# A fused decoder layer on one core: GpSimd's arithmetic given to VectorE and ScalarE, and ten chunks of x_m taken from the unnormalised input

## The chip, the cores and the metric

One core of a Trainium2 chip runs the whole layer in one launch. The core's engines run side by side, each through its own queue in order: TensorE (PE in the profile, PEld its weight loads), VectorE (DVE), ScalarE (ACT), GpSimd (POOL), and SyncE (SP), which here issues nearly all DMA transfers. The metric is the device time of one execution in microseconds (us), lower is better.

## What is computed

The layer normalises its input x (512 x 1024, float32), projects it with one matrix of 12288 columns, and feeds two branches: an attention over three dilated windows and an mLSTM with a causal convolution in front. Both are projected back, gated, added, projected once more and added to x, with a final RMSNorm. Cut to what the change touches:

```
xn = rmsnorm(x, norm_in_g)                       # x * rsqrt(mean(x*x) + eps) * g, a factor per token
q_a, k_a, v_a, z_a, x_m, z_m, o_m, gates = split(xn @ w_in)
# mLSTM branch
x_c  = silu(causal_depthwise_conv(x_m))          # 4 taps along time
q, k = block_diag_proj(x_c, wq), block_diag_proj(x_c, wk)     # blocks of 4 channels
v    = block_diag_proj(x_m, wv)
gate_pre = concat(q, k, v) @ w_if + b_if         # 8 columns: input and forget gates of 4 heads
h = mlstm_chunkwise(q, k, v, gates from gate_pre)
# attention branch: 16 heads of 64, scores q.k / 8 + bias(distance), softmax, times v
```

The factor of the normalisation belongs to a token, and tokens lie along the free axis of the projections that are held transposed. So the projection may also be made from x times the gain, and the result multiplied by the factor of each token.

## The kernel before

**Matmuls.** Every projection is made in three matmuls per 128 x 128 block: both operands are split into a high part (h, rounded to the fp32r format) and a low part (l, the rest), and hi*hi, hi*lo and lo*hi are added up in PSUM (`mm3`). For a chunk of 128 output channels a weight tile of 128 x 1024 is loaded (`raw`, 512 KB), ScalarE makes `whi`, VectorE makes `wlo` (`halves`), and TensorE runs 8 blocks x 3 matmuls of 512 columns. There are four buffers of each of raw, whi and wlo.

**Start.** x comes transposed in eight tiles `xt`. `x_split(k)` makes `xh` (ScalarE) and `xl` (VectorE) from xt and the gain. The first four chunks of x_m (`EARLY`) are taken from these unnormalised parts, `xu`, while the squares of x are summed and the token factors spread over the partitions into `rb` (a part of the tile `norm`). Then GpSimd multiplies the eight xt by rb, x_split runs on them again, and everything else uses these normalised parts `xh`, `xl`. The four early chunks are multiplied by rb when VectorE takes them out of PSUM; later chunks of x_m are copied out by ScalarE.

**The x_m loop** (16 chunks ct, four to a head). Per chunk: x_m to SBUF (tile `xm`) and to DRAM (`xmd`), a convolution of four steps on VectorE (`conv`: one tensor_scalar, three scalar_tensor_tensor), tanh on ScalarE (`cth`), one more VectorE step, the split (`xch`, `xcl`), a scaled copy (`sx`), then on TensorE `kp` (three matmuls with the folded matrix M of the q and k blocks, `Mh`, `Ml`), its split (`kph`, `kpl`, `kf`) and the products `S` (nine matmuls of 512, 384 and 256 columns and a small one). After each fourth chunk come 16 pairs of small matmuls `gates`, which need x_m and the convolution of all four.

**GpSimd's arithmetic before.** The eight products xt by rb; the folding of gate weights (`wrep`, `ust` in `fold_gates`), of `wqrep` and `mrow` (`fold_rows`), of `M` and `Bv` (`spread`, once per head each); in attention, per pair of heads, two copies of `qh` and two of `ql` to the other half of the partitions; and memsets and one cast, which stay.

**Order.** Nothing is written in the final order. `Recorder` notes every instruction with its inputs and outputs and then plays them through a list scheduler with its own costs per instruction: on each engine the ready instruction with the smallest priority goes first. Priority is the place in the program minus `R.ahead`, so a larger R.ahead pulls work forward (weights run 300 places ahead). The scheduled order is then fixed on each engine. Since one helper records everything, all lines of the profile read L333; the tiles' names tell the instructions apart. In the order, `x8` stands for eight like instructions in a row.

Of the kernel before, what the change touches and what calls it, by code (L numbers as in the profile page):

```python
# [11 lines left out]
F32 = mybir.dt.float32  # L12
F32R = mybir.dt.float32r
I32 = mybir.dt.int32
AF = mybir.ActivationFunctionType
OP = mybir.AluOpType

P = 128
T = 512
NT = T // P  # L20
D = 1024
NK = D // P
MW = 2048
NMT = MW // P
# [7 lines left out]
CQ, CK, CV, CZA, CXM, CZM, COM, CG = 0, 8, 16, 24, 32, 48, 64, 80  # L32
# [305 lines left out]
def hybrid_layer(ctx, tc, a, out):  # L338
    nc = tc.nc
    R = Recorder(nc, a["win"].tensor)  # L340
    V, A, PE, G, SP = (R.engine(e) for e in ("vector", "scalar", "tensor", "gpsimd", "sync"))
# [11 lines left out]
    def slot(name, dt=F32):  # L353
        return tile_of(upool, [P, 516], dt, name, "u", NSLOT)
# [24 lines left out]
    def dram(name, shape):  # L379
        return R.buf(lambda: dpool.tile(shape, F32, name=name), shape, F32, dram=True)  # L380

    def mm3(ps, lh, ll, rh, rl, first, last):
        PE.matmul(ps, lh, rh, start=first, stop=False)
        PE.matmul(ps, lh, rl, start=False, stop=False)
        PE.matmul(ps, ll, rh, start=False, stop=last)
# [42 lines left out]

    ident = const("ident", [P, P], F32)
    pc = const("pc", [P, PC_N], F32)  # L430
    EARLY = 4
    pair = [wide("xt") for _ in range(NK // 2)]
    xt = [pair[k // 2][:, k % 2 * T:k % 2 * T + T] for k in range(NK)]

# [9 lines left out]
    def proj_k(ps, hl, x, k):  # L444
        c = slice(k * P, (k + 1) * P)
        mm3(ps, hl[0][:, c], hl[1][:, c], *x[k], k == 0, k == NK - 1)
# [18 lines left out]
    xu = []  # L465
    early_ps = [mm_bank("xm") for _ in range(2)]
# [21 lines left out]
    norm = wide_t("norm", F32)  # L488
    rb, dg, ones = norm[:, :T], norm[:, T:2 * T], norm[:, 2 * T:2 * T + P]
# [17 lines left out]
    for c in range(2, EARLY):  # L507
# [2 lines left out]
        early_ps.append(sc_bank("xm"))  # L510
        for k in range(NK):
            proj_k(early_ps[c], early[c], xu, k)
    R.ahead = 1000
    xh, xl = [], []
    for k in range(NK):
        G.tensor_mul(xt[k], xt[k], rb)
        h, l = x_split(k)
        xh.append(h)
        xl.append(l)
    R.ahead = 0  # L520

    def proj_t(chunk, name):
        hl = weights(a["win"][chunk])
        ps = mm_bank(name)
        for k in range(NK):
            c = slice(k * P, (k + 1) * P)
            mm3(ps, hl[0][:, c], hl[1][:, c], xh[k], xl[k], k == 0, k == NK - 1)
        return ps

    def proj_n(chunk, name):  # L530
# [43 lines left out]
    def fold_gates():  # L574
        for m in range(2):
            G.memset(ust[m], 0.0)
        wrep = []
        for n in range(3):
            w = slot("wrep")[:, :512].rearrange("p (c o g) -> p c o g", c=NMT, o=4)
            SP.dma_start(w, a["wrep"][n])  # L580
            G.tensor_mul(w, w, brow[:, n, :, :, None].to_broadcast([P, NMT, 4, 8]))
            wrep.append(w)
        for m, ns in ((0, (0, 1)), (1, (2,))):
            u = ust[m][:, :, :8]
            parts = [wrep[n][:, :, o, :] for n in ns for o in range(4)]
            G.tensor_add(u, parts[0], parts[1])
            for x in parts[2:]:
                G.tensor_add(u, u, x)


    brow = const("brow", [P, 3, NMT, 4])
# [5 lines left out]
    def fold_rows():  # L597
        wq = slot("wqrep")[:, :256].rearrange("p (c i o) -> p c i o", c=NMT, i=4)
        SP.dma_start(wq, a["wqrep"])
        G.tensor_mul(wq, wq, brow[:, 1, :, None, :].to_broadcast([P, NMT, 4, 4]))  # L600
        G.tensor_add(mrow, wq[:, :, :, 0], wq[:, :, :, 1])
        G.tensor_add(mrow, mrow, wq[:, :, :, 2])
        G.tensor_add(mrow, mrow, wq[:, :, :, 3])

    def spread(rows, h, name):
        b = slot(name)[:, :512]
        G.tensor_mul(b.rearrange("p (c g i) -> p c g i", c=4, i=4),
                     rows[:, 4 * h:4 * h + 4, None, :].to_broadcast([P, 4, 32, 4]),
                     bmask[:, None, :, :].to_broadcast([P, 4, 32, 4]))
        return b  # L610
# [7 lines left out]
        return Mh, Ml  # L618

    fold_rows()  # L620
    xmd = dram("xmd", [NMT, P, T])
    sxd = dram("sxd", [NMT, P, T])
    v_of = {}

# [24 lines left out]
    sraw = []  # L649
    for ct in range(NMT):  # L650
        h, c = divmod(ct, 4)
        ps = early_ps[ct] if ct < EARLY else proj_t(CXM + ct, "xm")
        if c == 0:
            Mh, Ml = fold_qk(h)
            sps = [sc_bank("S") for _ in range(3)]
        m = slot("xm")[:, :T + 3]
        V.memset(m[:, 0:3], 0.0)
        if ct < EARLY:
            V.tensor_mul(m[:, 3:], ps, rb)
        else:  # L660
            A.activation(m[:, 3:], ps, AF.Copy)
        SP.dma_start(xmd[ct], m[:, 3:])
        if ct == 8:
            block_v(0)
        xc = conv_silu(m, ct)
# [236 lines left out]
    for p in range(HEADS_A // 2):  # L902
# [6 lines left out]
        for w in range(2):  # L909
            o, o2 = 64 * w, 64 - 64 * w  # L910
            src = qps[o:o + 64]
            A.activation(qh[w][o:o + 64], src, AF.Copy, scale=0.125)
            V.scalar_tensor_tensor(ql[w][o:o + 64], src, 0.125, qh[w][o:o + 64].bitcast(F32),
                                   op0=OP.mult, op1=OP.subtract)
            G.tensor_copy(qh[w][o2:o2 + 64], qh[w][o:o + 64])
            G.tensor_copy(ql[w][o2:o2 + 64], ql[w][o:o + 64])
        kps = proj_t(CK + p, "ka")
        kk = [slot("kk", F32R)[:, :T] for _ in range(2)]
        for w in range(2):
# [227 lines left out]
```

## Time and profile before

| what | value |
|---|---|
| median of 3 runs | 906.77 us (906.05 to 907.6) |
| the profiled execution | 907.21 us, span in the trace 905.2 us |
| TensorE busy | 886.7 us, 98% of the span |
| VectorE busy | 576.0 us, 64% |
| ScalarE busy | 385.8 us, 43% |
| GpSimd busy | 71.5 us, 8% |

The span runs from the first to the last instruction in the trace; the execution's time has about 2 us around it. "Busy" of an engine is the time in which at least one of its instructions runs. TensorE's matmuls overlap, so a row's duration (0.40 us for 512 columns) is longer than the distance to the next start (about 0.23 us), and work is counted by starts.

### The profile page before, as it was taken

Reading aid. Unit: us, or ns where it says so; the run is one execution under the profiler, and the core shown is the slowest. Engines: PE = TensorE matmul, PEld = TensorE weight load, DVE = VectorE, ACT = ScalarE, POOL = GpSimd, SP = SyncE. Lnnn points to the kernel's source line nnn. Section 1 sums busy time; section 2 is a strip of 40 time slices with the busy share of each in tenths; the row PEclk is TensorE's granted clock in tenths of the full one; section 3 lists DMA queues with packets and bytes.
Section 4 is the critical chain, followed back from the end, with each engine's and each line's share of the span. In section 5 each row is a group of like instructions: output and inputs, shape, how many; then the busy total and the mean of one; then the engine's idle time right before and its main releaser. Section 6 shows DMA issues by size and latency. Waiting matters only on the chain.

```text
span 905.2 us, 11844 instructions
## 1 busy us (share of the span) xinstructions
PE 886.7 (98%) x4340; PEld 727.1 (80%) x4340; DVE 576.0 (64%) x1154; ACT 385.8 (43%) x724; POOL 71.5 (8%) x136
## 2 busy tenths in 40 slices
PE   7899999999999999999999999999999999999997
PEld 5577878788878888887888888888888888888886
DVE  4998987785428546744855477874777843328533
ACT  7445544443343332332333265563665543325222
POOL 0950110000000000000000111101011100000000
PEclk9799999999999999999999999999999999999999
DMA  9652334233049234204313222313223223224221
GB/s 305 223 173 99 124 118 161 82 129 105 11 152 341 102 117 163 93 23 162 126 53 124 96 73 105 128 59 104 74 79 105 71 81 101 98 94 157 77 81 59
DMA packets 38801, 104.64 MB, mean 116 GB/s; under 512 B 4308, under 2 KB 6100, under 8 KB 38744
## 3 DMA queue, kind: packets, MB, share of 16 engines
q1 hardware_dynamic: 38600, 103.63, 33.6%
q8 instruction: 34, 0.56, 0.2%
q10 hardware_dynamic: 144, 0.26, 0.1%
q14 instruction: 23, 0.19, 0.1%
HBM read 93.35 MB, written 15.77 MB: 121 GB/s over the span
## 4 chain that ended last, share of the span: by engine, by line
PE 93%; DVE 4%; issue 1%; ACT 1%; DMA 1%; SPq 0%; DVEq 0%; ACTq 0%
PE zm L333 10%; PE gate L333 10%; PE ym L333 10%; PE om L333 9%; PE xm L333 8%; PE out L333 5%; PE qa L333 5%; PE za L333 5%; PE ka L333 5%; PE va L333 5%; PE ya L333 5%; PE num L333 3%; PE S L333 3%; PE pv L333 2%; PE sa L333 2%; PE pT L333 2%
## 5 line engine op out<-in xcount | busy, mean ns | idle before, releaser
L333 DVE TENSOR_TENSOR wlo<-raw,whi 128x1024 fp32r<-128x1024 f32 (+1 forms) x126 | 151.4, 1203 | 159.7 <-ACT whi L333 159.7
L333 ACT ACTIVATE whi<-raw 128x1024 fp32r<-128x1024 f32 (+1 forms) x126 | 128.1, 1019 | 284.7 <-PE zm L333 79.2
L333 PE MATMUL xm<-xh,whi 128*128 128x512 f32 x128 | 54.3, 427 | 5.2 <-ACT whi L333 5.2
L333 PE MATMUL xm<-xl,whi 128*128 128x512 f32 x128 | 54.0, 423 | 2.1 <-DVE xl L333 2.1
L333 PE MATMUL xm<-xh,wlo 128*128 128x512 f32 x128 | 53.2, 418 | 1.7 <-DVE wlo L333 1.7
L333 PE MATMUL om<-wlo,xh 128*128 128x512 f32 x128 | 50.9, 397 | 0.0
L333 PE MATMUL gate<-xh,whi 128*128 128x512 f32 x128 | 50.9, 397 | 0.0
L333 PE MATMUL zm<-xh,whi 128*128 128x512 f32 x128 | 50.8, 397 | 0.0
L333 PE MATMUL gate<-xl,whi 128*128 128x512 f32 x128 | 50.7, 396 | 0.0
L333 PE MATMUL om<-whi,xh 128*128 128x512 f32 x128 | 50.6, 396 | 0.0
L333 PE MATMUL om<-whi,xl 128*128 128x512 f32 x128 | 50.6, 395 | 0.0
L333 PE MATMUL gate<-xh,wlo 128*128 128x512 f32 x128 | 50.6, 395 | 0.0
L333 PE MATMUL ym<-yl,whi 128*128 128x512 f32 x128 | 50.5, 394 | 0.0
L333 PE MATMUL zm<-xl,whi 128*128 128x512 f32 x128 | 50.4, 394 | 0.0
L333 PE MATMUL ym<-yh,wlo 128*128 128x512 f32 x128 | 50.4, 394 | 0.0
L333 PE MATMUL zm<-xh,wlo 128*128 128x512 f32 x128 | 50.4, 394 | 0.0
L333 PE MATMUL ym<-yh,whi 128*128 128x512 f32 x128 | 50.2, 392 | 0.0
L333 ACT ACTIVATE p<-p,mx 128x128 f32<-128x128 f32 (+1 forms) x64 | 35.4, 556 | 14.3 <-DVE mx L333 14.3
L333 DVE CUSTOM_DVE_ANT_0 p<-sa,tb 128x128 f32<-128x128 f32 (+1 forms) x64 | 28.3, 488 | 18.2 <-PE sa L333 18.2
L333 DVE SCALAR_TENSOR_TENSOR conv<-xm,half,conv 128x512 f32<-128x512 f32 x48 | 37.2, 775 | 0.8
L333 DVE TENSOR_TENSOR ymacc<-ymacc,ym 128x512 f32<-128x512 f32 x24 | 16.5, 687 | 31.2 <-PE ym L333 31.2
L333 PEld LDWEIGHTS xm<-xh,whi 128*128 128x128 f32 x128 | 25.8, 201 | 11.6 <-ACT whi L333 5.8
(253 smaller groups left out, 2222.5 us busy)
## 6 DMA issues: line engine op xcount, KB each, us to landing
raw<-in_win_dram SPq DMA_DIRECT2D x94, 512.0 KB, 3.4
raw<-in_wpb_dram SPq DMA_DIRECT2D x16, 512.0 KB, 3.2
fr<-fd SPq DMA_DIRECT2D x1, 5120.0 KB
xmd<-xm SPq DMA_DIRECT2D x16, 256.0 KB, 2.2
sxd<-sx SPq DMA_DIRECT2D x16, 256.0 KB, 2.1
xmr<-xmd SPq DMA_DIRECT2D x16, 256.0 KB, 4.2
sxr<-sxd SPq DMA_DIRECT2D x16, 256.0 KB, 4.1
tb<-fr SPq DMA_DIRECT2D x16, 256.0 KB, 3.7
```

Source lines behind the costliest of these rows:

```text
L333: getattr(getattr(self.nc, op.eng), fn)(*a, **k)
```

## The change

Three things are changed.

First, all arithmetic of GpSimd goes elsewhere: the products xt by rb, the folds and `spread` to VectorE, the copies of qh and ql in attention to ScalarE. GpSimd keeps memsets and one cast.

Second, ten chunks of x_m (`UNNORMED`) instead of four are taken from the unnormalised parts `xu`; VectorE multiplies each by rb on its way out of PSUM. Only the first four (`EARLY`) are still made ahead of the loop, and their way out of PSUM is put forward by R.ahead = 5000.

Third, the normalisation of xt and its second split are no longer done at once: `normalise` is called for two of the eight tiles in each of the loop's turns 5 to 8 (`FIRST` and the three after it). The chunks from the eleventh on, and all later projections, use the normalised parts.

```
-    EARLY = 4
+    EARLY, UNNORMED, FIRST = 4, 10, 5
...
+    def x_m(ct, ps, norm=None):
+        m = slot("xm")[:, :T + 3]
+        V.memset(m[:, 0:3], 0.0)
+        if norm is None:
+            A.activation(m[:, 3:], ps, AF.Copy)
+        else:
+            V.tensor_mul(m[:, 3:], ps, norm)
+        SP.dma_start(xmd[ct], m[:, 3:])
+        return m
+
+    R.ahead = 5000
+    early_m = [x_m(c, early_ps[c], rb) for c in range(EARLY)]
+    R.ahead = 0
     xh, xl = [], []
-    for k in range(NK):
-        G.tensor_mul(xt[k], xt[k], rb)
+
+    def normalise(k):
+        V.tensor_mul(xt[k], xt[k], rb)
         h, l = x_split(k)
         xh.append(h)
         xl.append(l)
-    R.ahead = 0
...
-            G.tensor_mul(w, w, brow[:, n, :, :, None].to_broadcast([P, NMT, 4, 8]))
+            V.tensor_mul(w, w, brow[:, n, :, :, None].to_broadcast([P, NMT, 4, 8]))
...
-            G.tensor_add(u, parts[0], parts[1])
+            V.tensor_add(u, parts[0], parts[1])
...
-        ps = early_ps[ct] if ct < EARLY else proj_t(CXM + ct, "xm")
+        raw_x = ct < UNNORMED
+        ps = None if ct < EARLY else proj_t(CXM + ct, "xm", xu if raw_x else None)
+        if FIRST <= ct < FIRST + NK // 2:
+            normalise(2 * (ct - FIRST))
+            normalise(2 * (ct - FIRST) + 1)
...
+        R.ahead = EMPTY
+        m = early_m[ct] if ct < EARLY else x_m(ct, ps, rb if raw_x else None)
+        R.ahead = 0
...
-            G.tensor_copy(qh[w][o2:o2 + 64], qh[w][o:o + 64])
-            G.tensor_copy(ql[w][o2:o2 + 64], ql[w][o:o + 64])
+            A.activation(qh[w][o2:o2 + 64], qh[w][o:o + 64].bitcast(F32), AF.Copy)
+            A.activation(ql[w][o2:o2 + 64], ql[w][o:o + 64].bitcast(F32), AF.Copy)
```

The same exchange of G for V is made in `fold_rows` and `spread`.

VectorE's queue just behind the spreading of the token factors (`norm<-ident,nz` is the last step of that) stood like this before:

```order
L333 TENSOR_TENSOR xm<-xm,norm 128x512 x3
L333 CAST sel<-selr 36x512
L333 TENSOR_TENSOR rel_380<-relb,rel_380 32x16
L333 SCALAR_TENSOR_TENSOR xl<-xt,pc,xh 128x512
L333 TENSOR_TENSOR wlo<-raw,whi 128x1024
L333 SCALAR_TENSOR_TENSOR xl<-xt,pc,xh 128x512
L333 TENSOR_TENSOR wlo<-raw,whi 128x1024
L333 SCALAR_TENSOR_TENSOR xl<-xt,pc,xh 128x512 x2
L333 TENSOR_TENSOR wlo<-raw,whi 128x1024
L333 SCALAR_TENSOR_TENSOR xl<-xt,pc,xh 128x512 x4
```

and stands like this now, at the same place:

```order
L333 TENSOR_TENSOR xm<-xm,norm 128x512 x3
L333 TENSOR_TENSOR mrow<-wqrep 128x64
L333 TENSOR_SCALAR conv<-xm,half 128x512
L333 TENSOR_TENSOR mrow<-mrow,wqrep 128x64
L333 SCALAR_TENSOR_TENSOR conv<-xm,half,conv 128x512
L333 TENSOR_TENSOR wlo<-raw,whi 128x1024
L333 TENSOR_TENSOR mrow<-mrow,wqrep 128x64
L333 SCALAR_TENSOR_TENSOR conv<-xm,half,conv 128x512
L333 TENSOR_TENSOR xm<-xm,norm 128x512
L333 TENSOR_TENSOR wlo<-raw,whi 128x1024 x2
L333 TENSOR_TENSOR M<-mrow,bmask 128x512
```

The eight xl have gone from here; the first convolution and pieces of the folds have come in their place.

TensorE's queue at the start of the fifth chunk, with what each matmul waits for, stood like this before:

```order
L333 MATMUL xm<-xh,whi 128x512 [waits DVE_49,Activation_49]
L333 MATMUL xm<-xl,whi 128x512 [waits DVE_49]
L333 MATMUL xm<-xh,wlo 128x512 [waits DVE_49]
L333 MATMUL xm<-xh,whi 128x512 [waits Activation_49]
L333 MATMUL xm<-xl,whi 128x512 [waits DVE_49]
L333 MATMUL xm<-xh,wlo 128x512
```

and there it stands like this now:

```order
L333 MATMUL xm<-xh,whi 128x512 [waits DVE_49,Activation_49]
L333 MATMUL xm<-xl,whi 128x512
L333 MATMUL xm<-xh,wlo 128x512 [waits DVE_49]
L333 MATMUL xm<-xh,whi 128x512
L333 MATMUL xm<-xl,whi 128x512
```

The chunk no longer waits block by block for VectorE and ScalarE; it waits once for its weights. In the sixth chunk the first kp comes now, 14 matmuls behind the chunk's start (before, it came in the seventh):

```order
L333 MATMUL xm<-xl,whi 128x512
L333 MATMUL kp<-xch,Mh 128x512 [waits Activation_49]
L333 MATMUL xm<-xh,wlo 128x512
L333 MATMUL xm<-xh,whi 128x512
L333 MATMUL xm<-xl,whi 128x512
L333 MATMUL kp<-xcl,Mh 128x512 [waits DVE_49]
L333 MATMUL kp<-xch,Ml 128x512
```

So chains of the convolution start earlier between the x_m matmuls than before.

## Rows read from the trace of the kernel before

**Rows 1.** The page: busy time by engine, and TensorE's granted clock in 40 slices.

```profile
PE 886.7 (98%) x4340; PEld 727.1 (80%) x4340; DVE 576.0 (64%) x1154; ACT 385.8 (43%) x724; POOL 71.5 (8%) x136
...
PEclk9799999999999999999999999999999999999999
```

**Rows 2.** Windows: length, then busy PE, PEld, DVE, ACT, POOL; PEclk, DMA, GB/s.

```profile
31.53:76.95 45.42, 39.67 (x152) 30.05 (x150) 42.81 (x48) 21.36 (x34) 26.14 (x22) 0.85 0.48 164
76.95:160.00 83.05, 82.73 (x478) 66.71 (x478) 71.56 (x110) 41.23 (x79) 6.56 (x5) 1.00 0.36 128
```

**Rows 3.** The chain that ended last: start, duration in us, what.

```profile
505.29 5.57 PE qa L333 x24
```

**Rows 4.** Waits of TensorE: who for whom, total us, times, longest.

```profile
PE xm L333 <- DVE xl L333: 2.1, 3, 0.8
PE xm L333 <- DVE wlo L333: 1.7, 1, 1.7
PE aT L333 <- DVE aa L333: 0.5, 1, 0.5
```

**Rows 5.** Timeline of TensorE: start, duration in us, instruction, wait before it.

```profile
31.53 0.40 PE L333 MATMUL xm<-xh,whi 128*128 128x512 f32 x1
...
58.08 0.50 PE L333 MATMUL kp<-xch,Mh 128*128 128x512 f32 x1 [1.95 <-ACT xch L333]
...
59.57 0.63 PE L333 MATMUL xm<-xh,whi 128*128 128x512 f32 x1
60.00 0.63 PE L333 MATMUL xm<-xl,whi 128*128 128x512 f32 x1
...
76.95 0.41 PE L333 MATMUL gates<-xm,ust 128*32 128x256 f32 x2
...
100.67 0.41 PE L333 MATMUL gates<-xm,ust 128*32 128x256 f32 x2
```

**Rows 6.** VectorE by shape, 28.6 to 58.74: busy us, mean ns, idle before.

```profile
L333 DVE TENSOR_TENSOR wlo<-raw,whi 128x1024 fp32r<-128x1024 f32 x6 | 11.1, 1845 | 0.0
L333 DVE SCALAR_TENSOR_TENSOR xl<-xt,pc,xh 128x512 fp32r<-128x512 f32 x8 | 9.9, 1282 | 0.0
```

**Rows 7.** The same view of VectorE, 61.8 to 75.9.

```profile
L333 DVE TENSOR_TENSOR wlo<-raw,whi 128x1024 fp32r<-128x1024 f32 x2 | 2.5, 1225 | 0.7 <-ACT whi L333 0.7
```

**Rows 8.** Timeline of GpSimd.

```profile
26.84 13.06 POOL L333 TENSOR_TENSOR xt<-xt,norm 128x512 f32<-128x512 f32 x8 [0.77 <-DMA wrep<-in_wrep_dram]
```

**Rows 9.** Timeline of VectorE, seven instructions in a row while GpSimd rests.

```profile
85.86 0.75 DVE L333 SCALAR_TENSOR_TENSOR conv<-xm,half,conv 128x512 f32<-128x512 f32 x1
86.53 0.68 DVE L333 TENSOR_TENSOR xcl<-conv,xch 128x512 fp32r<-128x512 f32 x1
87.13 1.22 DVE L333 TENSOR_TENSOR wlo<-raw,whi 128x1024 fp32r<-128x1024 f32 x1
88.26 0.69 DVE L333 SCALAR_TENSOR_TENSOR conv<-cth,conv 128x512 f32<-128x512 f32 x1
88.89 0.56 DVE L333 TENSOR_TENSOR kpl<-kp,kph 128x384 fp32r<-128x384 f32 x1
89.36 0.48 DVE L333 TENSOR_SCALAR sx<-conv,hs 128x512 f32<-128x512 f32 x1
89.75 0.68 DVE L333 TENSOR_TENSOR xcl<-conv,xch 128x512 fp32r<-128x512 f32 x1
```

**Rows 10.** Timelines of VectorE and ScalarE before the fifth chunk.

```profile
26.80 1.89 DVE L333 TENSOR_TENSOR xm<-xm,norm 128x512 f32<-128x512 f32 x3 [1.66 <-ACT norm L333]
...
30.05 1.06 ACT L333 ACTIVATE whi<-raw 128x1024 fp32r<-128x1024 f32 x1 [1.16 <-DMA raw<-in_win_dram]
```

**Rows 11.** Attention: GpSimd's copies by shape, then timelines of ScalarE and TensorE.

```profile
L333 POOL CAST qh<-qh 64x512 fp32r<-64x512 f32 x16 | 10.8, 673 | 295.7 <-ACT qh L333 275.1 <-issue 20.1
...
540.42 1.06 ACT L333 ACTIVATE whi<-raw 128x1024 fp32r<-128x1024 f32 x1 [2.24 <-PE ka L333]
...
545.97 0.28 PE L333 MATMUL sa<-kk,qh 128*128 128x256 f32 x1
```

More of the change, by code (lines that the diff above doesn't have):

```diff
@@ L512, in hybrid_layer @@
             proj_k(early_ps[c], early[c], xu, k)
-    R.ahead = 1000
+    xmd = dram("xmd", [NMT, P, T])
+    def x_m(ct, ps, norm=None):
[10 more added lines that the diff above has]
+    R.ahead = 0
     xh, xl = [], []
-    for k in range(NK):
-        G.tensor_mul(xt[k], xt[k], rb)
+    def normalise(k):
+        V.tensor_mul(xt[k], xt[k], rb)
         h, l = x_split(k)
@@ L519, in hybrid_layer, with proj_t @@
         xl.append(l)
-    R.ahead = 0
-    def proj_t(chunk, name):
+    def proj_t(chunk, name, x=None):
         hl = weights(a["win"][chunk])
@@ L525, in proj_t @@
         for k in range(NK):
-            c = slice(k * P, (k + 1) * P)
-            mm3(ps, hl[0][:, c], hl[1][:, c], xh[k], xl[k], k == 0, k == NK - 1)
+            proj_k(ps, hl, x or list(zip(xh, xl)), k)
         return ps
@@ L585, in fold_gates @@
             parts = [wrep[n][:, :, o, :] for n in ns for o in range(4)]
-            G.tensor_add(u, parts[0], parts[1])
+            V.tensor_add(u, parts[0], parts[1])
             for x in parts[2:]:
-                G.tensor_add(u, u, x)
+                V.tensor_add(u, u, x)
     brow = const("brow", [P, 3, NMT, 4])
@@ L599, in fold_rows @@
         SP.dma_start(wq, a["wqrep"])
[L600 to L603, printed above, removed]
+        V.tensor_mul(wq, wq, brow[:, 1, :, None, :].to_broadcast([P, NMT, 4, 4]))
+        V.tensor_add(mrow, wq[:, :, :, 0], wq[:, :, :, 1])
+        V.tensor_add(mrow, mrow, wq[:, :, :, 2])
+        V.tensor_add(mrow, mrow, wq[:, :, :, 3])
     def spread(rows, h, name):
         b = slot(name)[:, :512]
-        G.tensor_mul(b.rearrange("p (c g i) -> p c g i", c=4, i=4),
+        V.tensor_mul(b.rearrange("p (c g i) -> p c g i", c=4, i=4),
                      rows[:, 4 * h:4 * h + 4, None, :].to_broadcast([P, 4, 32, 4]),
@@ L620, in hybrid_layer @@
     fold_rows()
-    xmd = dram("xmd", [NMT, P, T])
     sxd = dram("sxd", [NMT, P, T])
@@ L655, in hybrid_layer @@
             sps = [sc_bank("S") for _ in range(3)]
[L656 to L662, printed above, removed]
+        R.ahead = EMPTY
+        m = early_m[ct] if ct < EARLY else x_m(ct, ps, rb if raw_x else None)
+        R.ahead = 0
         if ct == 8:
```

## The prediction, made before the changed kernel ran

> **What bounds the kernel now.** I read the page's busy shares and slices first. TensorE is busy 98% of the span, VectorE 64%, ScalarE 43%, GpSimd 8%, and the clock granted to TensorE is below full only near the start [rows 1]. So TensorE sets the end, and only time in which it waits or runs slowly can be won. The change keeps every matmul, so TensorE's own work does not move.
>
> The windows by stage then say where TensorE loses. From 31.53, where the fifth chunk of x_m begins, to 76.95, where the first group of gates matmuls begins, it is busy 39.67 of 45.42 us at a granted clock of 0.85; in the next stretch the clock is 1.00 [rows 2]. At full clock 24 matmuls of 128x512, one chunk, take 5.57 us, 0.232 each [rows 3]. By the order the stage holds 108 x_m matmuls, 9 of kp and the S of three chunks. 117 x 0.232 = 27.1 us. S of a chunk is three matmuls each of 512, 384 and 256 columns and a small one; in proportion to columns 1.75 us, in all 5.3. That is 32.4 us of work in 45.4: **13.0 us are lost here, the most the change can give.** They go to waits for xl and wlo at the start [rows 4], to the half clock (1.2 instead of 2.4 GHz) that follows them, to 1.95 us of waiting for xch at 58.08, and to the half clock that follows that (matmuls 0.43 apart from 59.57) [rows 5].
>
> Who is late? VectorE: busy 42.81 of the 45.42 us [rows 2]. But its instructions are long there. Between 28.6 and 58.74, without a pause, a wlo takes 1845 ns and an xl 1282 on average [rows 6]; after 61.8 a wlo takes 1225 [rows 7]. In that time GpSimd multiplies eight xt (from 26.84 to 39.9) [rows 8] and folds the gate weights. So GpSimd's arithmetic stretches VectorE's, and VectorE holds TensorE back.
>
> **Prices on an undisturbed VectorE**, as starts apart [rows 9]: conv step 0.67, two-tile product (xcl) 0.60, wlo 1.13, last conv step 0.63, kpl 0.47, sx 0.39; the first conv step, a tensor_scalar as sx is, 0.45, an estimate a little above sx's.
>
> **What is freed.** The instructions of 28.6 to 58.74 take 30.1 us. At these prices: 6 wlo 6.8, 8 xl 5.4, 4 conv steps, Ml and a last step 3.9, xm and xcl 1.2, 2 first steps and sx 1.3, two small casts 0.5: 19.1. Freed: 11.0 us.
> The Trainium skill, page SBUF — State Buffer, section Who interferes with whom, calls this an exclusive lock between a GpSimd instruction that reads SBUF and a VectorE instruction with two SBUF inputs, and exempts one with a single such input. By that rule the stretch ends with GpSimd's arithmetic. The trace agrees: three xm<-xm,norm, with one input in PSUM, take 1.89 us together while GpSimd runs [rows 10].
>
> **What is added to VectorE.** Before the first gates group: 4 xt (2.4), 4 more xm (2.4), 3 wrep (1.8), wqrep, mrow and M (1.4), 10 sums of gate weights, ust (2.0): 10.0 us. An ust of 128 strided columns has no VectorE row: between 0.15 (a quarter of a two-tile product) and 0.47 (kpl, three times its columns); I take 0.2, nearest to the quarter; the other end adds 2.7 us, kept for the range. Gone or moved behind that group: 8 xl (5.4), two casts (0.5), one wlo (1.1). Net 3.0 us more, against 11.0 freed.
>
> **The walk.** Before 26.8 nothing differs, and the loads are issued in the same order, so the fifth chunk's whi is done at 31.1 as now [rows 10].
> 1. VectorE does three xm by 28.7 and small pieces, waits for whi, and ends wlo at 32.3. TensorE's third matmul, due at 32.0, waits 0.35. It needs no xl of the normalised input: those waits are gone.
> 2. The chunk ends at 37.5; 14 matmuls on, at 40.7, comes the first kp. VectorE has by then done 3 more wlo, 2 xm, M, the conv steps and Ml; last conv step at 40.4, ScalarE's xch at 41.2. Wait 0.5 us.
> 3. xcl 41.9, a wrep, five ust, kpl 44.8; TensorE, with x_m between, needs it at 44.9. No wait.
> 4. From 44.8 to chunk 3's last conv step, which the first gates need: 5 ust 1.0, 3 first steps 1.35, 9 steps 6.0, 3 last ones 1.9, 3 xm 1.8, 3 wlo 3.4, 2 sx, 2 xcl and 2 kpl 2.9, 4 xt 2.4: 20.8 us, and 0.5 for pauses between dependent neighbours: 66.1. **The gates begin at 66.2.** TensorE alone would be there at 31.53 + 32.4 + 0.85 = 64.8, and loses the other 1.4 in small pieces at kp and S. Against 76.95 [rows 5] that is 10.7 us earlier with the same work done (205 x_m matmuls instead of 204).
> 5. Counted on the same way, VectorE without a pause (8 xl, 4 xt, four chunks' conv, 2 wlo) reaches the last conv step before the second gates group at 96.2, and TensorE by its own work at 96. It begins at 96.3, against 100.67 [rows 5], with 24 x_m and 4 S matmuls more behind it (6.1 us): 10.5 us ahead.
> 6. From about 106 TensorE has x_m in stock while VectorE catches up (now it is busy 71.56 of 83.05 us there [rows 2]). After 160 TensorE's clock is full [rows 1], and its order in attention is the old one. The 10.5 us stay to the end.
>
> **Edits taken at nothing.** The other xt products and the split of the normalised x come at 70 to 96, under chunks 8 and 9. The eleventh chunk reads them from 88 to 96, each ready 0.1 to 0.5 us ahead: thin cover, counted in rival A. Without the cover each of 16 instructions of 0.6 shows, 10 us. The xmd writes of six more chunks wait for VectorE, not ScalarE, in SyncE's queue, with raw loads behind them; a load is issued three chunks ahead, and 5 us late would still be in time. Bv on VectorE (0.6 each) has om and ym matmuls beside it. In attention four copies per pair of heads go from GpSimd (673 ns) to ScalarE; at the same price 2.7 us per pair. They end by 540, sa needs them at 545.97, and ScalarE is idle 2.24 us before 540.42 [rows 11]. Without that cover they cost 8 x 2.7 = 22 us.
>
> **Sum.** The profiled execution took 907.21 (span 905.2, 2.0 around it). 907.21 - 10.5 = 896.7; the median of the runs is 0.44 lower: **896.3**.
>
> **Rivals.**
> A. VectorE slips in the lockstep from 38 to 98: dear ust sums (2.7 us), or a wait of some 2 us at a kp that brings the half clock as after 58.08, where from 59.57 to 63.5 some 2 us were lost. One such wait with its fall is 4 us; with some of the dear sums 5.5, so 901.8; a slip alone 899. For it: margins of 0.1 to 0.5 us. Against: the wait of 0.5 for aT [rows 4] shows no fall of the clock. Chance 0.2.
> B. The other side: the stretch belongs to a busy stage (DMA, ScalarE), not to GpSimd; it stays, and takes the moved instructions too. Then the first gates come at 66.2 + 11.0 + 0.8 x 10.0 = 85.2, 8.3 us later than now: 915. It decides if a two-tile instruction at 30 to 55 us still takes above 1.2 us. Against it: the unstretched xm rows in that time, and a wlo of 1225 ns as soon as GpSimd rests. Chance 0.05.
> The Trainium skill, page Perfetto Trace Analysis, section Optimizing Scalar/DVE Operations, would give work of a saturated VectorE to ScalarE or even GpSimd, the reverse of this change, though it adds that between VectorE and GpSimd this might not help; by its first half B's 915 would come, by its second the forecast. VectorE's rows beside GpSimd bear out the second.
> C. The stretch stays on the old instructions alone: 66.2 + 11.0 = 77.2, 0.3 later than now; or the gain comes back as a wait for the gate sums behind 160. 905 to 908. Chance 0.05.
> D. ScalarE's copies push back the exponentials in attention: with all of the 22 us shown, 918; with half, 907. Chance 0.03.
>
> **Chances.** Forecast 0.67 (893.3, where TensorE waits for nothing, to 898); A 0.2; B, C, D as said. The range takes in the forecast's bounds and A to its worst: 893.3 to 901.8. A measurement of this kernel tells about 0.2%, 1.8 us, from no change: faster by more 0.87, within 0.05, slower 0.08.
>
> **What will show it.** Right: no wait for xl at 31 to 41; granted clock near 1.00 from 31 to 77; wlo at 1.2 us and two-tile products at 0.68 throughout; first gates near 66, second near 96; TensorE's attention rows unmoved. Wrong: a kp wait of 2 us with slow matmuls behind it (A), long VectorE rows at 30 to 55 (B), early first gates but no earlier end (C), pT waiting for p (D).

## The result, and the profile of the changed kernel

The changed kernel takes **895.58 us** (median of 4 runs, 894.47 to 896.43), the kernel before 906.41 on the same chip (905.8 to 907.6). The ratio is 0.9878, with a 95% interval of 0.9861 to 0.9895: 10.8 us, or 1.2%, faster. The forecast was 896.3. The profiled execution of the changed kernel took 894.47 us, span 892.5.

The page, with the lines that answer to [rows 1]:

```profile
PE 879.0 (98%) x4340; PEld 723.0 (81%) x4340; DVE 573.9 (64%) x1193; ACT 402.2 (45%) x750; POOL 11.2 (1%) x71
...
POOL 0000000000000000000000000000000000000000
PEclk9999999999999999999999999999999999999999
```

VectorE has 39 instructions more than before and yet 2.1 us less busy time. The seven tenths that the granted clock showed in the second slice is gone.

The windows of the changed kernel, cut at 31.53, at its first gates group and at 150, answer to [rows 2] (length, then busy PE, PEld, DVE, ACT, POOL; PEclk, DMA, GB/s):

```profile
31.53:65.14 33.61, 32.39 (x150) 26.14 (x148) 32.47 (x57) 15.32 (x23) 0.00 (x0) 1.00 0.58 211
65.14:150.00 84.86, 84.86 (x490) 68.61 (x490) 80.90 (x134) 44.83 (x85) 0.38 (x2) 1.00 0.36 128
```

The stretch up to the first gates is 33.6 us long instead of 45.4, TensorE idles 1.22 us in it instead of 5.75, and runs at 2.4 GHz throughout (1.00 instead of 0.85). VectorE is still busy nearly all of that time, but 57 of its instructions run in it, against 48 in the longer stretch before.

TensorE's waits answer to [rows 4] (who for whom, total us, times, longest):

```profile
PE xm L333 <- ACT whi L333: 5.2, 1, 5.2
PE kp L333 <- ACT xch L333: 1.2, 1, 1.2
PE aT L333 <- DVE aa L333: 0.5, 1, 0.5
```

Its timeline has one idle row in the stretch, which answers to the one at 58.08 in [rows 5]:

```profile
41.01 0.50 PE L333 MATMUL kp<-xch,Mh 128*128 128x512 f32 x1 [1.22 <-ACT xch L333]
41.34 0.39 PE L333 MATMUL xm<-xh,wlo 128*128 128x512 f32 x1
```

The waits for xl and wlo are gone. (The wait of 5.2 us for whi is the program's start and is as long in the kernel before.) The kp wait of 1.22 us has a matmul 0.33 us behind it and then 0.23 between matmuls: no fall of the clock.

TensorE's rows of the tile gates show where a group begins; the first one (count, ns min/median/max, first and last start):

```profile
L333 PE MATMUL gates<-xm,ust x16: 377/378/404, 65.1 to 66.7; 128*32 128x256 f32 x16
```

The four groups start at 65.14, 95.15, 125.87 and 152.12 us now, and at 76.95, 100.67, 129.85 and 164.28 before. These times can't be set against each other as they stand, because the order ahead of a group differs. So I count, for every kernel below, the work that TensorE's order puts ahead of a group (matmuls times their spacing at full clock: 0.232 us for 512 columns [rows 3], less in proportion for fewer, 0.105 for a gates matmul), and take it from the group's start. What is left is **TensorE's lag**: all that it lost up to there, the program's start included. Its size depends on these prices, so only differences between kernels are read from it.

| kernel | first gates | work ahead | lag | lag at the fourth | median us |
|---|---|---|---|---|---|
| before | 76.95 | 54.9 | 22.0 | 22.3 | 906.41 |
| after | 65.14 | 55.2 | 10.0 | 9.9 | 895.58 |

The lag falls by 12.0 us by the first group and by 12.4 by the fourth, and the spans differ by 12.7. So nearly everything is won before 65 us and nothing is given back. That the medians differ by 10.8 and the two profiled executions by 12.7 is scatter: the profiled execution of the changed kernel is the fastest of its four.

### The profile page after: what moved, and what is told of

Same layout as the page of the kernel before. It is cut to its first block, busy times and chain, and to the rows that moved or that the text cites. A ratio compares the mean times of both kernels' runs of the same rounds, so it can differ in the third digit from the quotient of the medians.

```text
span 892.5 us, 11773 instructions
## 1 busy us (share of the span) xinstructions
PE 879.0 (98%) x4340; PEld 723.0 (81%) x4340; DVE 573.9 (64%) x1193; ACT 402.2 (45%) x750; POOL 11.2 (1%) x71
## 4 chain that ended last, share of the span: by engine, by line
PE 93%; DMA 3%; DVE 1%; ACT 1%; SPq 0%; issue 0%; ACTq 0%; DVEq 0%
PE zm L333 10%; PE gate L333 10%; PE ym L333 10%; PE om L333 9%; PE xm L333 7%; PE out L333 5%; PE qa L333 5%; PE va L333 5%; PE ya L333 5%; PE ka L333 5%; PE za L333 5%; PE num L333 3%; PE S L333 3%; PE pv L333 2%; PE sa L333 2%; PE pT L333 2%
## 5 line engine op out<-in xcount | busy, mean ns | idle before, releaser
L333 DVE TENSOR_TENSOR wlo<-raw,whi 128x1024 fp32r<-128x1024 f32 (+1 forms) x126 | 147.4, 1173 | 156.1 <-ACT whi L333 156.1
L333 PE MATMUL xm<-xh,whi 128*128 128x512 f32 x128 | 52.0, 411 | 5.2 <-ACT whi L333 5.2
L333 PE MATMUL xm<-xh,wlo 128*128 128x512 f32 x128 | 51.3, 402 | 0.0
L333 PE MATMUL xm<-xl,whi 128*128 128x512 f32 x128 | 51.1, 401 | 0.0
L333 ACT ACTIVATE p<-p,mx 128x128 f32<-128x128 f32 (+1 forms) x64 | 35.4, 556 | 14.6 <-DVE mx L333 14.6
L333 PEld LDWEIGHTS xm<-xh,whi 128*128 128x128 f32 x128 | 24.4, 192 | 10.9 <-ACT whi L333 5.5
## 6 DMA issues: line engine op xcount, KB each, us to landing
fr<-fd SPq DMA_DIRECT2D x1, 5120.0 KB, 22.4
```

Of the source, the lines that this page charges most:

```text
L333: getattr(getattr(self.nc, op.eng), fn)(*a, **k)
```

## Experiments

All ratios below are to runs of the kernel before on the same chip; its medians there were 906.41 to 907.04 us, so medians of different kernels can be set against each other only to some 0.6 us. Theory S of the prediction is: GpSimd's reads of SBUF stretch VectorE's instructions with two SBUF operands, and VectorE paces TensorE up to the first gates.

### Does GpSimd's arithmetic stretch VectorE by itself?

Three probes put GpSimd work into the changed kernel that nobody waits for. In the first two the traces show TensorE, VectorE and ScalarE run the instructions of the changed kernel in the same order from start to end, in the third up to 103 us; so only what GpSimd does beside them differs. The first reads:

```
+    G.tensor_mul(dg, rb, rb)
+    for _ in range(15):
+        G.tensor_mul(dg, rb, rb)
```

> The kernel after, plus 16 products of GpSimd over 128x512 that read a tile in SBUF twice and write a scratch tile that nobody reads. They need only the token factors and so run from about 26 to about 52 us; nobody waits for them. The order of TensorE and of VectorE in that stretch is that of the kernel after. Theory S (a GpSimd product that reads SBUF stretches VectorE's instructions with two SBUF operands): wlo 1.4 to 2.3 us instead of 1.22, conv steps 1.3 to 1.8 instead of 0.74, xm<-xm,norm unchanged at 0.68; waits of 2 to 4 us at the first kp with slow matmuls behind; first gates 5 to 9 us later than 65.1; 900 to 906. Rival N (what GpSimd cost before was only that TensorE and VectorE waited for its results): all rows as in the kernel after, 895 to 896.5.

Measured: **906.08 us** (905.18 to 907.64), ratio to before 1.000 [0.9991, 1.001]. The whole gain is gone, though every instruction that was moved is still moved. GpSimd's timeline (16 products from 26.52 to 49.81):

```profile
26.52 23.29 POOL L333 TENSOR_TENSOR norm<-norm 128x512 f32<-128x512 f32 x16 [24.55 <-ACT norm L333]
```

VectorE's timeline beside them and just behind them:

```profile
28.73 1.35 DVE L333 TENSOR_SCALAR conv<-xm,half 128x512 f32<-128x512 f32 x1
...
34.54 1.11 DVE L333 TENSOR_TENSOR mrow<-mrow,wqrep 128x64 f32<-128x64 f32 x1
35.57 1.61 DVE L333 SCALAR_TENSOR_TENSOR conv<-xm,half,conv 128x512 f32<-128x512 f32 x1
37.10 0.68 DVE L333 TENSOR_TENSOR xm<-xm,norm 128x512 f32<-128x512 f32 x1
37.71 3.44 DVE L333 TENSOR_TENSOR wlo<-raw,whi 128x1024 fp32r<-128x1024 f32 x2
...
43.96 2.06 DVE L333 TENSOR_TENSOR wlo<-raw,whi 128x1024 fp32r<-128x1024 f32 x1
...
48.83 1.52 DVE L333 TENSOR_TENSOR wrep<-wrep,brow 128x512 f32<-128x512 f32 x1
50.28 0.47 DVE L333 TENSOR_SCALAR sx<-conv,hs 128x512 f32<-128x512 f32 x1
50.67 0.68 DVE L333 TENSOR_TENSOR xcl<-conv,xch 128x512 fp32r<-128x512 f32 x1
51.27 0.68 DVE L333 TENSOR_TENSOR wrep<-wrep,brow 128x512 f32<-128x512 f32 x1
```

A wrep takes 1.52 us at 48.83 while GpSimd still works, and 0.68 at 51.27 when it rests. The xm<-xm,norm at 37.10, one operand in PSUM, takes its 0.68 in the middle of it. Theory S is too narrow in one point: a first conv step, a tensor_scalar with one SBUF operand, is stretched too (1.35 us at 28.73; 0.54 in the changed kernel). TensorE then waits 2.6 us for wlo and 4.8 us at the first kp, and the first gates come at 76.3 instead of 65.14 with the same 55.2 us of work ahead.

The second probe writes and hardly reads:

```
+    G.tensor_mul(dg, rb, rb)
+    for _ in range(46):
+        G.memset(dg, 0.0)
```

> The kernel after, plus one product of GpSimd and 46 memsets of GpSimd over 128x512 that only write a scratch tile and are to last about as long as the 16 products of the other probe. Theory S (it is the reading of SBUF that counts): rows of VectorE as in the kernel after, first gates at 65 to 66, 895 to 897. Rival U (any running GpSimd instruction, or any load on SBUF, stretches VectorE): as the probe that reads, 900 to 906, conv steps above 1.2 us.

Measured: **895.46 us** (894.86 to 896.24), ratio 0.9882 [0.9866, 0.9899]. GpSimd by shape between 20 and 80 us (count, then busy us, mean ns | idle before):

```profile
L333 POOL MEMSET norm<- 128x512 f32 x46 | 25.1, 546 | 2.6
```

VectorE by shape between 28.6 and 58.74:

```profile
L333 DVE TENSOR_TENSOR wlo<-raw,whi 128x1024 fp32r<-128x1024 f32 x6 | 7.3, 1216 | 1.0 <-ACT whi L333 0.9
L333 DVE SCALAR_TENSOR_TENSOR conv<-xm,half,conv 128x512 f32<-128x512 f32 x9 | 6.7, 739 | 0.0
L333 DVE TENSOR_SCALAR conv<-xm,half 128x512 f32<-128x512 f32 x4 | 2.4, 591 | 0.0
L333 DVE TENSOR_SCALAR sx<-conv,hs 128x512 f32<-128x512 f32 x3 | 1.9, 627 | 0.0
```

GpSimd is busy even longer than in the first probe (25.1 us against 22.1), yet wlo and the conv steps keep their price to within 2 ns (1217 and 741 in the changed kernel). Only the tensor_scalar instructions are touched (591 and 627 ns, against 537 and 475). So what costs time is not that GpSimd is busy, but that it reads. The rivals N and U fall.

A third probe reads one operand instead of two: behind one product, 30 times `G.tensor_copy(dg, rb)`.

> The probe with 16 products of GpSimd again, but behind the first product 30 copies over 128x512, which read one operand in SBUF instead of two; nobody waits for them. Theory S1 (any GpSimd instruction that reads SBUF stretches VectorE's instructions with two SBUF operands): conv steps and wlo longer than 0.74 and 1.22 as long as the copies run, first gates 3 to 11 us later than 65.1; 898 to 906. Theory S2 (only GpSimd instructions with two SBUF operands do): rows and gates as beside the memsets; 895 to 897.

Measured: **904.74 us** (903.01 to 905.07), ratio 0.9971 [0.9958, 0.9984]. The copies run from 27.45 to 55.9. VectorE's timeline beside them:

```profile
38.85 1.09 DVE L333 SCALAR_TENSOR_TENSOR conv<-xm,half,conv 128x512 f32<-128x512 f32 x1
39.87 1.62 DVE L333 TENSOR_TENSOR wlo<-raw,whi 128x1024 fp32r<-128x1024 f32 x1
41.42 0.68 DVE L333 TENSOR_TENSOR xm<-xm,norm 128x512 f32<-128x512 f32 x1
```

So S1 holds: a copy, which reads one operand, stretches too, and by less than a product, which reads two. TensorE waits 4.9 us at two kp for xch and 1.3 for wlo, and its lag is 20.0.

### Which of the moved pieces count?

The attention copies back on GpSimd (the two `A.activation` lines undone), all else as in the changed kernel:

> The changed kernel with only the copies of qh and ql in attention back on GpSimd; the orders of TensorE, VectorE and SyncE are the same, word for word. Both theories: no difference, ratio to the changed kernel within 0.1%, 894.7 to 896.5, since sa comes 6 us behind the copies in either. If the copies did matter (GpSimd's reads stretch VectorE in attention too), above 897.5.

Measured: **895.35 us** (894.9 to 895.67), ratio 0.9875 [0.9859, 0.989], gates at 65.03 to 152.02: no difference. These copies were worth nothing either way.

The folds back on GpSimd (wrep, ust, wqrep, mrow, M and Bv with `G.` again; xt and the copies stay moved):

> The changed kernel with only the folds back on GpSimd (wqrep, mrow, wrep, ust, M, Bv); the xt products stay on VectorE. VectorE is relieved of 5.8 us of work before the first gates, and GpSimd works some 20 us between 23 and 57. Theory S with the stretch of the kernel before (11.0 us lost to VectorE beside some 30 us of GpSimd, 0.37 per us): 7.4 lost against 5.8 relieved, first gates at 66 to 68, 896 to 898.5. Theory U (VectorE's load, not stretch): first gates at or before 65, 893 to 895.

Measured: **899.03 us** (898.45 to 899.69), ratio 0.9916 [0.99, 0.9932]: 3.4 us above the changed kernel, somewhat above theory S. The last piece of the folds in GpSimd's timeline:

```profile
32.74 7.26 POOL L333 TENSOR_TENSOR ust<-ust,wrep 128x128 f32<-128x128 f32 x7
```

TensorE's idle rows from the fifth chunk, which begins at 31.83, up to the first gates:

```profile
33.91 0.50 PE L333 MATMUL xm<-xh,wlo 128*128 128x512 f32 x1 [1.47 <-DVE wlo L333]
43.01 0.50 PE L333 MATMUL kp<-xch,Mh 128*128 128x512 f32 x1 [1.20 <-ACT xch L333]
```

These folds end at 40.0. The price is a lag of 12.7 instead of 10.0 at the first gates. Of the difference 1.1 us are there as the fifth chunk begins (in the changed kernel at 30.72), and 1.5 are the wait for wlo; the kp wait of 1.20 us the changed kernel has too (1.22). The clock falls behind neither. By the fourth group the lag is 14.6 instead of 9.9, some 2 us more; the later folds, one per head, are the likely cause, which no run parts from others.

All arithmetic back on GpSimd, with the ten unnormalised chunks kept:

> The changed kernel with all of GpSimd's arithmetic back on GpSimd (folds, xt products one by one, the copies in attention); ten chunks from the unnormalised input stay. Theory S: VectorE's two-tile instructions are stretched again while GpSimd works (wlo above 1.6 us on average from 28 to 58), the first gates matmuls come 5 to 9 us later than the 65.1 of the changed kernel, and the time is 900 to 905. Theory U: no stretch that matters, 894.5 to 897.

Measured: **907.12 us** (906.32 to 909.19), ratio 1.0009 [0.9999, 1.0018]. Theory U falls, and S was too mild. VectorE by shape from 28.6 to 53:

```profile
L333 DVE TENSOR_TENSOR wlo<-raw,whi 128x1024 fp32r<-128x1024 f32 x5 | 7.9, 1604 | 0.0
L333 DVE SCALAR_TENSOR_TENSOR conv<-xm,half,conv 128x512 f32<-128x512 f32 x4 | 5.2, 1292 | 0.0
```

TensorE's longest idle row behind the program's start:

```profile
49.37 0.50 PE L333 MATMUL kp<-xcl,Mh 128*128 128x512 f32 x1 [2.81 <-DVE xcl L333]
```

So ten unnormalised chunks alone give nothing: they free TensorE from xl, and the stretched VectorE then makes it wait at wlo and kp instead.

### Is the move enough without the unnormalised chunks?

The kernel before with all the arithmetic moved, four unnormalised chunks, the second split at once:

> The kernel before, with all of GpSimd's arithmetic moved to VectorE and ScalarE, but still four chunks of x_m from the unnormalised input and the normalisation done at once. Theory S (VectorE was late because GpSimd stretched it, and that is most of the loss): the stretch is gone (a wlo at 1.22 us between 28 and 58), but the eight xt products and the xl now stand ahead of the fifth chunk's wlo in VectorE's queue, so TensorE waits some 4.5 us there and runs at half clock for some 4 us more: 5 to 7 of the 10.8 us gained are kept, 899.5 to 901.5. Theory U (the gain is that the fifth to tenth chunks don't wait for the normalised input; where the arithmetic runs matters little): 905 to 908, as before.

Measured: **908.6 us** (907.14 to 909.81), ratio 1.0019 [1.0009, 1.0028], so the move alone is a little slower than before: S of that run is wrong by some 8 us. No VectorE row is stretched any more, and yet TensorE stands still for 10.5 us. Its timeline there:

```profile
41.59 0.77 PE L333 MATMUL xm<-xh,whi 128*128 128x512 f32 x1 [10.50 <-DVE xm L333]
42.15 0.63 PE L333 MATMUL xm<-xl,whi 128*128 128x512 f32 x1
42.58 0.63 PE L333 MATMUL xm<-xh,wlo 128*128 128x512 f32 x1
```

The VectorE row that releases it:

```profile
40.75 0.69 DVE L333 TENSOR_TENSOR xm<-xm,norm 128x512 f32<-128x512 f32 x1
```

The fifth chunk needs a PSUM bank, which an early chunk of x_m frees when VectorE multiplies it by rb. In VectorE's queue that product stands behind eight xt, eight xl and three wlo. Behind the wait TensorE runs at the lower of its two levels, 1.2 GHz: matmuls 0.43 us apart.

Is it the bank alone? The same kernel with the early chunks taken out of PSUM first, as in the changed kernel (the copies of later chunks out of PSUM are also put forward as there, by R.ahead = 300). Its edit, against the changed kernel:

```
-    EARLY, UNNORMED, FIRST = 4, 10, 5
+    EARLY, UNNORMED = 4, 4
...
+    R.ahead = 1000
+    for k in range(NK):
+        normalise(k)
+    R.ahead = 0
...
-        if FIRST <= ct < FIRST + NK // 2:
-            normalise(2 * (ct - FIRST))
-            normalise(2 * (ct - FIRST) + 1)
```

> All of GpSimd's arithmetic moved, and the four early chunks taken out of PSUM ahead of everything else, as in the kernel after; but only those four unnormalised, and the second split at once, as in the kernel before. It parts two readings of the kernel with the work moved alone (908.6). Theory S (there the fifth chunk waited 10 us for a PSUM bank that stood behind 19 instructions in VectorE's queue): that wait goes; instead TensorE waits for xl and wlo, since VectorE still has 8 xt, 8 xl (about 10.5 us) ahead of the wlo, which ends at about 39 to 40: 4 to 6 us of waits from 31 to 41 and slow matmuls behind; VectorE has some 6 us more to do before the first gates than in the kernel after, so these come at 70 to 73; 900 to 904. Rival T (the second split at once costs as much as all that was freed, wherever the bank is freed): first gates at 76 to 79, 906 to 909.

Measured: **911.68 us** (911.51 to 912.07), ratio 1.006 [1.0045, 1.0075]. The place of the wait moves, as S says, and its size fits, but the time doesn't: it lies above T's range too. Some of TensorE's idle rows:

```profile
39.63 0.79 PE L333 MATMUL xm<-xh,wlo 128*128 128x512 f32 x1 [5.77 <-DVE wlo L333]
...
136.35 0.49 PE L333 MATMUL kp<-xch,Mh 128*128 128x512 f32 x1 [1.44 <-ACT xch L333]
...
138.78 0.50 PE L333 MATMUL S<-xch,kph 128*128 128x512 f32 x1 [0.98 <-ACT kph L333]
```

The VectorE rows that the first of them waits for:

```profile
37.75 0.68 DVE L333 TENSOR_TENSOR xt<-xt,norm 128x512 f32<-128x512 f32 x1
38.36 1.22 DVE L333 TENSOR_TENSOR wlo<-raw,whi 128x1024 fp32r<-128x1024 f32 x1
```

Here wlo stands behind 15 products and splits. The lag at the first gates is 18.5 us, 3.5 better than before. But the scheduler, which moves everything when one thing moves, has put two more chunks of x_m ahead of these gates (66.5 us of work instead of 55.2). They are missing later: from 136 to 140, where TensorE waits at kp and S with slow matmuls behind, no x_m matmul runs in between; and another 3.0 us of small waits come behind 160, where the kernel before has 0.7. The lag at the fourth group is 23.5.

Does TensorE have to need the normalised parts for that? The changed kernel with its ten unnormalised chunks, but the eight products and second splits at once, which nobody needs before the eleventh chunk:

> The kernel after, ten chunks unnormalised, but the eight products xt and the eight xl at once, before the loop, where nobody needs them until the eleventh chunk. Theory S (the place in VectorE's queue counts, not TensorE's need of the normalised parts): the fifth chunk's wlo stands behind 3 xm, 8 xt, 4 xl and another xm and ends at about 38; TensorE waits some 6 us at its third matmul, slow matmuls behind; more x_m ahead of the first gates and too little left later; 902 to 908. Rival V (once TensorE needs no normalised part, the 16 instructions cost nothing): no wait above 1 us at the fifth chunk; 895 to 897.

Measured: **913.32 us** (912.09 to 913.77), ratio 1.0066 [1.0051, 1.0081]. Rival V falls. TensorE's idle rows at the fifth chunk:

```profile
34.20 0.51 PE L333 MATMUL xm<-xh,whi 128*128 128x512 f32 x1 [1.90 <-ACT whi L333]
38.33 0.80 PE L333 MATMUL xm<-xh,wlo 128*128 128x512 f32 x1 [3.40 <-DVE wlo L333]
```

It is the place in VectorE's queue that counts: 8 xt and 4 xl that nobody needs yet stand ahead of the wlo that TensorE needs now. The time is above S's range for the same reason as in the run before: 78.4 us of work ahead of the first gates, then no x_m matmul from 126 to 148, and waits at kp of 3.4 and 1.6 us at 133 and 142.

### How many chunks, and when is the second split?

Only the numbers in `EARLY, UNNORMED, FIRST` are changed: to 4, 6, 2, to 4, 8, 4, and to 4, 12, 7.

> The kernel after with six unnormalised chunks instead of ten, and the normalisation and second split in the loop's turns 2 to 5 instead of 5 to 8. Theory S (VectorE paces the stretch up to the first gates): with about 16 more instructions of 0.6 to 0.7 us there (10 us) and 2 xm less, VectorE is late again at kp or at xl; first gates 3 to 8 us later than 65.1; 898 to 903. Rival V (VectorE has room up to the first gates, only the start of the fifth chunk was the trouble): first gates at 65 to 66.5, 895 to 896.5.

> The kernel after with eight unnormalised chunks instead of ten, the normalisation and second split in turns 4 to 7. With six (turns 2 to 5) it gave 906.9: TensorE waited 2.8 us for xh at 50.5, as the seventh chunk started. Theory S (each unnormalised chunk gives VectorE 5.6 us more until the split is needed; two more chunks move that need from 47.6 to about 59): waits for xh and xl of 0 to 2 us in all, 896 to 901. Rival: eight are as good as ten, 895 to 896.5.

> The kernel after with twelve unnormalised chunks instead of ten, the normalisation and second split in turns 7 to 10. Theory S (ten already leave no wait for xh or xl): nothing to win, two xm more on VectorE, two xm copies less on ScalarE, which the stage can bear; 895 to 896.5. Rival: VectorE still holds TensorE back between 65 and 125 in small pieces; 892 to 894.5.

Measured: six **906.91 us** (ratio 1.0004 [0.9993, 1.0015]), eight **905.41** (0.9979 [0.997, 0.9988]), twelve **897.22** (0.9893 [0.9876, 0.9909]), ten as said 895.58 (0.9878). The times lie above theory S's ranges in all three; six and eight lose nearly everything. TensorE's timeline with six:

```profile
47.38 0.39 PE L333 MATMUL xm<-xh,wlo 128*128 128x512 f32 x1
50.55 0.49 PE L333 MATMUL xm<-xh,whi 128*128 128x512 f32 x1 [2.77 <-ACT xh L333]
```

And with eight:

```profile
47.20 0.40 PE L333 MATMUL xm<-xh,wlo 128*128 128x512 f32 x1
51.97 0.80 PE L333 MATMUL kp<-xch,Mh 128*128 128x512 f32 x1 [4.38 <-ACT xch L333]
```

Between S of the first chunk and kp of the second, from 45.2 to 51.24 us, the changed kernel runs 26 x_m matmuls, 6.0 us of work that waits for nothing. With eight chunks five matmuls stand there, and TensorE then waits 4.38 us; with six there are seven ahead of a wait for xh, the normalised input. In both, the granted clock falls behind the wait (0.52 from 50 to 60 us with eight, 0.83 with six). The mechanism for six was as expected; with eight it was not xh but the order: no matmul of the next x_m chunk stands ahead of that kp, and where the chunk does start, its first matmul waits for VectorE, which by the order frees its PSUM bank late (the next x_m to be taken out of PSUM comes at 56.67 us, in the changed kernel at 46.68). Whether another order would make eight as good was not tried.

None of these versions beats the changed kernel; the one with the attention copies back equals it.

### All lags side by side

| kernel | lag at the first gates | at the fourth | median us |
|---|---|---|---|
| attention copies back | 9.9 | 9.8 | 895.35 |
| after | 10.0 | 9.9 | 895.58 |
| after + memsets | 10.4 | 10.6 | 895.46 |
| twelve chunks | 10.9 | 10.4 | 897.22 |
| folds back | 12.7 | 14.6 | 899.03 |
| after + copies | 20.0 | 20.3 | 904.74 |
| eight chunks | 20.9 | 21.4 | 905.41 |
| after + products | 21.1 | 21.0 | 906.08 |
| before | 22.0 | 22.3 | 906.41 |
| six chunks | 22.1 | 22.4 | 906.91 |
| ten chunks alone | 22.2 | 23.5 | 907.12 |
| move alone | 23.5 | 22.9 | 908.6 |
| move alone, PSUM first | 18.5 | 23.5 | 911.68 |
| ten chunks, split at once | 16.9 | 26.5 | 913.32 |

Down to the move alone, the lag at the first gates tells the time: it and the median, each taken from that of the changed kernel, agree within 1.3 us. The last two rows show its limit: there TensorE got to the gates with less lag by using up x_m work that it lacked later.

## Why the prediction was right, point by point

**The bound and the most to be won.** 13.0 us were said to be lost between 31.53 and 76.95. The lag fell by 12.0 up to the first gates, but 0.8 of that is there as the fifth chunk begins. So some 11.2 of the 13.0 were won in the stretch: TensorE now takes 34.4 us (30.72 to 65.14) for 32.6 us of work.

**The stretch and its prices.** Right. VectorE by shape in the changed kernel, 28.6 to 58.74, answers to [rows 6]:

```profile
L333 DVE SCALAR_TENSOR_TENSOR conv<-xm,half,conv 128x512 f32<-128x512 f32 x10 | 7.4, 741 | 0.0
L333 DVE TENSOR_TENSOR wlo<-raw,whi 128x1024 fp32r<-128x1024 f32 x6 | 7.3, 1217 | 1.6 <-ACT whi L333 1.6
L333 DVE TENSOR_TENSOR xm<-xm,norm 128x512 f32<-128x512 f32 x4 | 2.7, 681 | 0.0
L333 DVE TENSOR_SCALAR conv<-xm,half 128x512 f32<-128x512 f32 x4 | 2.1, 537 | 0.0
L333 DVE TENSOR_TENSOR ust<-ust,wrep 128x128 f32<-128x128 f32 x8 | 1.9, 280 | 0.0
```

A wlo takes 1217 ns instead of 1845. The rule quoted from the Trainium skill (page SBUF — State Buffer, section Who interferes with whom: two SBUF inputs against a GpSimd instruction that reads SBUF, not one that only writes) now has direct runs behind it: a conv step of 1.52 to 1.61 us beside products, 1.09 to 1.18 beside copies, 0.74 beside memsets. By the same section a tensor_scalar, in the modes in which it takes both port pairs, contends with GpSimd also without a read; the trace agrees here too: sx 627 ns beside memsets, 475 without. The prediction's "exempts one with a single such input" left this condition out: the exemption held for xm<-xm,norm (0.68 us throughout), and not for the first conv step (1.35 us beside products, 0.54 alone).

**The one price without a row, ust,** was taken as 0.2 between 0.15 and 0.47. Three in a row take 0.68 us from 42.82 to 43.50, so 0.2 apart: right.

**Step 1 of the walk** was wrong by a little: the fifth chunk's third matmul, the first that needs wlo, starts at 31.21 without a wait, where 32.0 and a wait of 0.35 were said. The chunk begins 0.8 us earlier than before (30.72 instead of 31.53). ScalarE's whi for it began at 28.83, not at 30.05 [rows 10], and VectorE's three xm at 26.13, not at 26.80. The walk's "before 26.8 nothing differs" was not quite so: wqrep and one wrep now run on VectorE from 25.20 to 26.13, in time in which it waited before. Part of the 0.8 us is scatter of the start: in the other four kernels with the same order there (the three probes and the one with the attention copies back) the fifth chunk begins at 30.99 to 31.30.

**Step 2**, the first kp: xch was forecast for 41.2 and kp came at 41.01. The wait, 1.22 instead of 0.5, is longer only because TensorE arrived earlier, at 39.8. No slow matmuls came behind it, which was the open point of rival A.

**Step 3**: xcl ends at 41.89 (41.9 forecast), kpl at 43.98 (44.8 forecast), no wait: right.

**Steps 4 and 5**: first gates at 65.14 (66.2 forecast), second at 95.15 (96.3 forecast). Both are 1.1 early. VectorE, which the walk follows there, was 0.8 early at kpl already, and took 20.8 us from there to the last conv step (64.75) where 21.3 were said. TensorE's losses in the stretch, set down at 0.85 and 1.4 us, came to 1.8; the walk's 32.4 us of work lack one x_m matmul (0.23), which it names itself (205 instead of 204).

**Step 6**, that the gain stays: right; lag differences 12.0, 11.7, 12.3 and 12.4 at the four gates groups, 12.7 at the end.

**Edits taken at nothing.** No wait for xt or xh at the eleventh chunk. In attention ScalarE's copies cost 631 ns each, 673 on GpSimd [rows 11], and sa at the place of [rows 11] waits for nothing; with the copies back on GpSimd the time is the same.

**The sum.** 10.5 us were forecast; the medians differ by 10.8, the profiled executions by 12.7. The walk was made on profiles, and by them it is 2.2 us short, of which 0.8 is the earlier start that no step has. That the median came within 0.7 us of 896.3 is in part luck: the profiled execution of the changed kernel lies 1.1 us below its median, that of the kernel before 0.8 above.

**The rivals.** A (slips in the lockstep) did not come, but it was near: eight chunks instead of ten, a wait of 4.4 us at a kp with the lower clock behind it, lose 9.8 of the 10.8 us. Its price, 898 to 901.8, was too low for such a case: that kernel takes 905.4. B (the stretch belongs to a busy stage) is ruled out by the changed kernel, where the stage is as busy and wlo takes 1217 ns, and by the probe that reads. C (given back later) and D (attention) are ruled out by the lags and by the kernel with the copies back.

**What the prediction did not see.** It counted the freed time of VectorE as the cause and the unnormalised chunks as removed waits for xl, step by step, in the one order that it had. It priced neither part alone. Read as two gains to be added, that would have been wrong: by the ratios the move alone is 1.7 us slower than before, the ten chunks alone 0.8 (not to be told from none), and both together are 11.0 faster. Either one leaves a wait of 2.8 to 10.5 us before the first gates, at another place, and the lower clock behind most of them.

The expectations of the runs were less good than the prediction, and all in one direction: nine of the twelve kernels came out slower than theory S said for them (the probe that reads by 0.1 us only). In two the first wait was priced about right (5.8 us in 4 to 6 for the early chunks taken first; 5.3 of about 6 for the split at once), and what the new order did later was left out. In others the wait itself was missed: 10.5 us where 4.5 were said for the move alone, 4.4 where 0 to 2 were said with eight chunks.

## What to carry to other kernels

When VectorE holds TensorE back, compare its rows while GpSimd works with the same rows while it rests: if those with two SBUF operands are longer and those with one operand in PSUM are not, suspect GpSimd's reads; a probe that reads a tile for nobody, beside one that only writes, shows whether they are the cause and what they cost. Giving the work back to VectorE pays only if what TensorE needs next does not queue behind it: so put work that nobody needs yet (here the second split) where its user is, and give TensorE enough matmuls that wait for nothing. Price a change of order in the order itself, and count a kernel's lag (time less work done) rather than the time of a landmark.

## What the runs showed of the hardware that was not expected

**Beside one kind of GpSimd instruction the stretch is much the same amount for instructions of different sizes, not a factor.** Beside products of GpSimd a 128x64 mrow goes from 0.27 to 1.11 us, a 128x512 wrep from 0.68 to 1.52, a 128x1024 wlo from 1.22 to 2.06 (the one at 43.96 us): 0.84 more for each of the three sizes. A few pay less: two wlo in a row 3.44 us instead of some 2.36, an Ml 0.92 instead of 0.68. Beside copies the conv step pays 0.35 to 0.44 and wlo 0.40. The products run 1.46 us apart there (23.29 us for 16), and a wrep and its successor start 1.45 apart: the two engines seem to take turns, one instruction each. That reading is argued from the spacing, not shown on its own. So small instructions suffer most: an mrow costs four times its price. The amount goes with what GpSimd runs. VectorE's rows in the kernel before, first beside the products xt, then beside sums of gate weights (ust):

```profile
32.56 2.29 DVE L333 TENSOR_TENSOR wlo<-raw,whi 128x1024 fp32r<-128x1024 f32 x1
...
48.19 1.48 DVE L333 TENSOR_TENSOR wlo<-raw,whi 128x1024 fp32r<-128x1024 f32 x1
```

That is 1.07 and 0.26 us more than the 1.22 alone. The 1845 ns of [rows 6] are a mean over wlo of 1.42 to 2.30 us.

**GpSimd's busy share says nothing of its price.** 16 products, busy for 22.1 us or 2.4% of the span, cost 10.5 us of kernel time, and 30 copies 9.2; 46 memsets, 25.1 us, cost nothing.

**A wait of TensorE costs its own length, and some waits also the slow matmuls behind them.** Waits of 1.20, 1.22, 1.33 and 1.47 us had matmuls 0.23 us apart soon behind them; behind waits of 2.6, 2.77, 4.38, 5.77 and 10.50 us the next matmuls come 0.43 apart (1.2 GHz), for some 3 us after the one of 2.6 and for 8.4 after the one of 4.38 (51.97 to 60.38, with two more waits of 0.2 and 0.6 in it), which at half the pace is 1.5 and 4.2 us more. Behind the wait of 2.81 at 49.37, and behind that of 1.95 in the kernel before [rows 5], four or five matmuls start 0.23 to 0.36 apart, and only then 0.43. Shorter waits close together have slow matmuls behind them too: 0.77, 1.72 and 0.85 us between 31.9 and 36.6 in the kernel before [rows 4].
